# Ten instead of seven pairs of up-projection tiles by seven products of quarters, with the later gated results kept in 32 bits until the down projection

## The chip, the cores and the metric

The kernel runs on one core of one Trainium2 chip. The metric is the device time of one execution in microseconds (us). The kernel before the change took 720.85 us, the median of three runs (719.79 to 722.53).

## The reference, cut to what matters

One decoder layer on `x` of 512 rows and 1024 columns: a token mixer (attention and a state-space scan), a layer norm, and a gated feed-forward part with a second layer norm. The change sits in the feed-forward part, and its scheduling rule reaches the mixer too.

```python
def conv_ffn(h, w_up, conv_w, conv_b, w_down):
    u = causal_dwconv(h @ w_up, conv_w, conv_b)
    g, val = jnp.split(u, 2, axis=-1)
    return (jax.nn.silu(g) * val) @ w_down
...
        h = x * (1.0 + sc2) + sh2
        y = conv_ffn(h, ffn_up_w[i], ffn_conv_w[i], ffn_conv_b[i], ffn_down_w[i])
        x = layer_norm(DEEPNORM_ALPHA * x + (1.0 + g2) * y, ln2_g[i], ln2_b[i])
```

`w_up` is 1024 x 5632: 22 gate tiles and 22 value tiles of 128 columns. `w_down` is 2816 x 1024.

## The kernel before, in words

**Precision.** Every large product is made in three matmuls of a reduced 32-bit type: each operand is split into a high part (`hi`, a copy on ACT) and a low part (`lo`, a subtraction on DVE), and `mm3` multiplies high by high, high by low and low by high. In the trace `wh` and `wl` are the parts of a weight tile, `h2h` and `h2l` those of the normed input, and the two halves of a `mid` tile those of a gated result.

**Up stage.** The 22 pairs (a gate tile `i = 0` and a value tile `i = 1` of one `j`) are made one after the other. A direct pair takes 2 x 8 x 3 = 48 matmuls of 128 x 512 (`up` in the trace). A pair in the list `SEVEN` (before: j = 3, 5, ..., 15) treats weights and input as 2 x 2 quarters and takes seven products of quarters instead of eight: 7 x 4 x 3 = 84 matmuls of 128 x 256 (`sP`, in four PSUM banks). It wants four extra sums of weight quarters (`sw`, DVE), seven splits of weight quarters (`wq`: ACT, then DVE), two copies (`m`, ACT) and seven sums of results (DVE, on `sP` and `u`). The sums of the input (`TS`, name `ts`) are made once and held in four of the six buffers of class "e".

**After a pair.** `up_post` runs a three-tap convolution (one ACT and two DVE instructions per tile), a SiLU on ACT and the product on DVE. In the kernel before it then splits the result at once into a `mid` tile (ACT, then DVE), which the down stage reads.

**Down stage.** `by_tile` makes the output in two passes over the two column halves. Each pass goes through 11 weight items, each of which serves two values of j; an item is 24 matmuls of 128 x 512 for all four row tiles (`dn`). `ln2` adds the residual: `x_back` brings the normed rows back from DRAM into two "e" buffers (`XN`), `row_loads` scales and shifts them on POOL (16 instructions, key `res`), and `ln2` wants them when the first pass ends.

**What sets the order.** The program is written by a greedy planner (`Order`, lines 48 to 300). Work is given as threads; at each step the planner estimates when the next instruction of each thread could start (`start`, `price`) and emits the earliest, with priorities. The result is one fixed order for each engine. Which parts of a tile depend on each other is told by `touch`: for a large SBUF tile by blocks of 128 columns, and before the change for every PSUM tile as one whole (the key set is `{0}`), so that a reader of a part counts as waiting for all that is written to the bank. This is the planner's picture only. The waits in the program are set apart from it, by the framework. Buffers come from classes ("e": 6, "b": 25) and quotas (`R.limit`): `w2` is the number of weight parts of the up stage that may be held, `raw` the number of loaded weight tiles. All loads are issued by SP, in one queue.

Line 300 of the profile is the planner's `emit`, so all instructions share that line and are told apart by the names of their tiles.

Of the kernel before, what the change touches and what calls it, by code (L numbers as in the profile page):

```python
# [9 lines left out]
F32 = mybir.dt.float32  # L10
F32R = mybir.dt.float32r
# [5 lines left out]
P = 128  # L17
SEQ = 512
# [25 lines left out]
class Region:  # L44


    def __init__(self, base=0.0):
        self.base, self.wr, self.rd, self.psum = base, {}, {}, False

    def end(self):  # L50
        return max([self.base] + [v[0] for v in self.wr.values()] + [v[0] for v in self.rd.values()])
# [56 lines left out]
class Order:  # L108
# [37 lines left out]
    def try_alloc(self, a):  # L146
        if a.after:
            if self.due(a) > self.time:
                return None
            a.after = ()  # L150
        pool, slots = self.pools[a.cls]
        group = a.group or a.cls
        if self.used.get(group, 0) >= self.quota.get(group, 1000):
            return None
        free = [s for s in slots if s["free"]]
        if not free:
            return None
        s = min(free, key=lambda q: q["end"])
        t = pool.tile(a.shape, a.dt, name=self.name(a.name), tag=s["tag"], bufs=1)
        s["free"] = False  # L160
        self.used[group] = self.used.get(group, 0) + 1
        self.regs[t.tensor.name] = Region(s["end"])
        self.regs[t.tensor.name].psum = a.cls == "ps"
        self.owner[t.tensor.name] = (s, group)
        return t

# [7 lines left out]
    def touch(self, ap):  # L174
        name = ap.tensor.name
        if name not in self.regs:
            return None
        if name.startswith("dr"):
            return name, [(0, 0)]
        dims = [tuple(d) for d in ap.ap]  # L180
        pitch = max(dims[0][0], 1)
        p0, off = divmod(ap.offset, pitch)
        n = dims[0][1] if dims[0][0] else 1
        if pitch <= self.GRAIN or self.regs[name].psum:
            chunks = {0}
        else:
            starts = [off]
            for st, cnt in dims[1:-1]:
                starts = [s + st * i for s in starts for i in range(cnt if st else 1)]
            st, cnt = dims[-1] if len(dims) > 1 else (0, 1)  # L190
            chunks = {c for s in starts for c in range(s // self.GRAIN, (s + st * (cnt - 1)) // self.GRAIN + 1)}
        keys = [(h, c) for h in range(p0 // 64, (p0 + n - 1) // 64 + 1) for c in chunks]
        return name, keys
# [211 lines left out]
def layer_kernel(  # L405
# [274 lines left out]
            rows_item(w_out, k, n)  # L680
    UP0 = len(items)
    NSPLIT = 4
    SEVEN = [3, 5, 7, 9, 11, 13, 15]
    for j, i in up_tiles:
        cols_item(w_up, i * D_FF + j * P)
    for n in range(2):
# [547 lines left out]
            R.free(XN[t // 2])  # L1234

    def x_back():
        yield Need("tsfree")
        for h in range(2):
            XN[h] = yield buf("e", [P, 2, DM], "XN")
            for i in range(2):  # L1240
                yield S.dma_start(XN[h][:, i], xn_d[2 * h + i])
                R.mark(("back", 2 * h + i))
# [79 lines left out]


    MID, U, E8 = {}, {}, {}
    MTAGS = ["b"] * 12 + ["e"] * 8 + ["b"] * 2

    def conv3(ps, dst, ch, neg):
        f0, f1, f2 = (nfw[:, i, ch - NFF:ch - NFF + 1] if neg else w[:, ch:ch + 1] for i, w in enumerate((fw0, fw1, fw2)))
# [5 lines left out]
    def up_post(j, i, ps, neg=False):  # L1334
        u = yield buf("s", [P, SEQ], "u")
        yield from conv3(ps, u, j + 22 * i, neg)
        if i == 0:
            yield A.activation(u, u, AF.Silu)
            U[j] = u
            R.mark(("u", j))  # L1340
            return
        yield Need(("u", j))
        g = U.pop(j)
        yield V.tensor_mul(g, g, u)
        R.free(u)
        if MTAGS[j] == "b":
            mid = yield buf("b", [P, 2, SEQ], "mid", "mid", F32R)
        else:
            if j % 2 == 0:
                E8[j] = yield buf("e", [P, 2, 2, SEQ], "mid2", dt=F32R)  # L1350
                R.mark(("mid2", j))
            yield Need(("mid2", j - j % 2))
            mid = E8[j - j % 2][:, j % 2]
        yield A.activation(mid[:, 0], g, AF.Copy)
        yield V.tensor_sub(mid[:, 1], g, mid[:, 0].bitcast(F32))
        R.free(g)
        MID[j] = mid
        R.mark(("mid", j))


    RES = {}
# [246 lines left out]
    def seven(j):  # L1608

        h2h, h2l = H2["hl"]  # L1610
        for _ in range(2):
            w_next()
        ps = []
        for i in range(2):
            ps.append((yield bank("gemm", "sP")))

        def b(k0, c):
            return h2h[:, k0:k0 + 4, c], h2l[:, k0:k0 + 4, c]

        def t(m):  # L1620
            return TS[m][:, 0], TS[m][:, 1]

        yield Need("ts")

        for m, p, c, (rh, rl) in ((0, 0, L, b(0, L)), (1, 1, L, t(0)), (2, 0, H, t(1)), (4, 1, H, t(2)),
                                  (5, 2, L, b(4, L)), (6, 3, L, t(3)), (3, 2, H, b(4, H))):
            if p == len(ps):
                ps.append((yield bank("gemm", "sP")))
            yield Need(("ws", j, m))
            w = WS.pop((j, m))  # L1630
            lead[0] += 2 / 7
            for k in range(4):
                yield mm3(ps[p][:, c], w[:, 0, k], w[:, 1, k], rh[:, k], rl[:, k], k == 0, k == 3)
            R.free(w)
            if m == 0:
                R.spawn(seven_out(j, ps), 2)
            R.mark(("sm", j, m))
# [26 lines left out]
    def ffn():  # L1664
        h2h, h2l = H2["hl"]
        pend = []
        for part in range(2):
            c0, c1 = part * 256, part * 256 + 256
            for j, i in up_tiles[:NSPLIT]:
                if part == 0:  # L1670
                    key, n_ = w_next()
                    ps = yield bank("gemm", "up")
                    yield Need(key)
                    w = W.pop(n_)
                    pend.append((ps, w))
                else:
                    ps, w = pend.pop(0)
                for k in range(KC):
                    yield Need(("h2", 2 * part, k // 4), ("h2", 2 * part + 1, k // 4))
                    yield mm3(ps[:, c0:c1], w[0][:, k], w[1][:, k], h2h[:, k, c0:c1], h2l[:, k, c0:c1],  # L1680
                              k == 0, k == KC - 1)
                if part == 1:
                    R.free(*w)
                    R.spawn(up_post(j, i, ps), 2)
        R.free(ROWS.pop("g1p"))
        R.limit(raw=3, w2=10, gemm=8)
        for n, (j, i) in enumerate(up_tiles[NSPLIT:]):
            if j in SEVEN:
                if i == 0:
                    yield from seven(j)  # L1690
                if j == SEVEN[-1] and i == 1:
                    R.free(*TS)
                    R.mark("tsfree")
                    R.limit(w2=7)
                continue
            key, n_ = w_next()
            ps = yield bank("gemm", "up")
            yield Need(key)
            w = W.pop(n_)
            for k in range(KC):  # L1700
                yield mm3(ps, w[0][:, k], w[1][:, k], h2h[:, k], h2l[:, k], k == 0, k == KC - 1)
            R.free(*w)
            R.spawn(up_post(j, i, ps), 2)
        R.free(h2h, h2l)
        RES["rw"] = yield buf("h", [P, 4, DM], "RW")
        RES["w"] = yield buf("h", [P, 4, 2, 512], "wlast", dt=F32R)
        R.mark("fin")
        R.limit(gemm=8, w2=8)
        ps = {}
        cuts = [[(0, 512), (512, DM)]] * 3 + [[(0, 512), (512, 768), (768, DM)]]  # L1710
        for n in range(2):
            for t in range(NT):
                for c in cuts[t][1:] if n else cuts[t][:1]:
                    ps[t, c[0]] = yield bank("gemm", "dn")
                if n == 0:
                    R.spawn(ln2(t, ps, cuts[t]), 0.5 if t == NT - 1 else 1)

            def block(i, tile, w):
                t, (c0, c1) = tile
                s, c = slice(t * P, (t + 1) * P), slice(c0 - n * 512, c1 - n * 512)  # L1720
                for b in range(2):
                    k = 2 * i + b
                    yield Need(("mid", k))
                    yield mm3(ps[t, c0][:, :c1 - c0], MID[k][:, 0, s], MID[k][:, 1, s],
                              w[0][:, b, c], w[1][:, b, c], k == 0, k == NFF - 1)

            tiles = [(t, c) for t in range(NT) for c in (cuts[t][1:] if n else cuts[t][:1])]
            yield from by_tile(tiles, NFF // 2, (1, LATE_DN)[n], block, lambda tile: ("y2", tile[0], tile[1][0]))
# [30 lines left out]
    R.spawn(ada_last(), 8)  # L1759
    R.spawn(quarters(), 1.5)  # L1760
    R.spawn(x_back(), 6)
    R.run()


# [28 lines left out]
```

## Time and profile before

| | us |
|---|---|
| median of three runs (lowest, highest) | 720.85 (719.79, 722.53) |
| profiled execution: device time | 723.08 |
| profiled execution: span | 721.3 |
| busy PE / DVE / ACT / POOL in the span | 703.3 / 584.5 / 342.3 / 58.5 |

The span runs from the first to the last instruction of the profiled execution; 1.78 us of its device time lie around it. Busy times are unions of an engine's instructions. PE matmuls overlap in the records, so a PE that is shown busy may still have small gaps in it. In the chain of waits a row such as `408.36 9.95 PE sP L300 x84` is a stretch of time (start, length, engine, tile name, line, number of instructions).

### The profile page before, as it was taken

The numbers are of one execution on the slowest core, as the hardware profiler recorded it, in microseconds if no ns is written. First come the engines' busy times: TensorE is split into PE (matmuls) and PEld (weight loads), VectorE is DVE, ScalarE is ACT, GpSimd is POOL, SyncE is SP. The second block draws the span as 40 slices with busy tenths as digits, with TensorE's granted clock in tenths as the row PEclk, the third lists the DMA queues.
The fourth block names the chain that finished last, engine by engine and source line by source line (L and its number), as shares of the span: only waits on it lengthen the run. The fifth ranks groups of instructions, "written<-read, shape, count | busy, mean of one in ns | idle before, by whom it ended". The sixth has DMA issues, their size and how long they took to land.

```text
span 721.3 us, 10347 instructions
## 1 busy us (share of the span) xinstructions
PE 703.3 (98%) x3873; PEld 589.1 (82%) x3873; DVE 584.5 (81%) x1072; ACT 342.3 (47%) x605; POOL 58.5 (8%) x71
## 2 busy tenths in 40 slices
PE   8999999999999899999999999999999999999995
PEld 7787887888778787878998888999988888888885
DVE  5879989999898889678899999999985663247646
ACT  2347578655665364323775655556554352211200
POOL 0010012100000000000100000000000019200023
PEclk9999999999999999999999999999999999999998
DMA  8997083063556415654533432444383345322202
GB/s 264 307 286 231 0 264 93 2 175 101 176 162 221 130 30 174 218 190 147 164 100 108 127 98 79 144 149 146 112 268 89 94 153 179 100 88 75 100 30 87
DMA packets 112323, 102.12 MB, mean 142 GB/s; under 512 B 3732, under 2 KB 93200, under 8 KB 112273
## 3 DMA queue, kind: packets, MB, share of 16 engines
q1 hardware_dynamic: 112273, 101.47, 46.0%
q8 instruction: 30, 0.49, 0.3%
q14 instruction: 20, 0.16, 0.1%
HBM read 97.22 MB, written 4.23 MB: 141 GB/s over the span
## 4 chain that ended last, share of the span: by engine, by line
PE 64%; DVE 18%; DMA 6%; SPq 4%; ACT 4%; issue 3%; POOL 0%; DVEq 0%; ACTq 0%
PE up L300 19%; PE dn L300 17%; PE sP L300 9%; PE po L300 7%; PE fm L300 7%; SPq L300 4%; DVE wl L300 3%; DMA ad<-in_ada_w_dram 3%; DVE acc L300 2%; DMA aw<-in_ada_w_dram 2%; DVE Y L300 1%; DVE pr L300 1%; ACT csb L300 1%; DVE u L300 1%; DMA csb<-drcs 1%
## 5 line engine op out<-in xcount | busy, mean ns | idle before, releaser
L300 DVE TENSOR_TENSOR wl<-raw,wh 128x1024 fp32r<-128x1024 f32 x88 | 110.8, 1262 | 51.3 <-ACT wh L300 51.2
L300 ACT ACTIVATE wh<-raw 128x1024 fp32r<-128x1024 f32 x88 | 91.9, 1053 | 83.7 <-PE dn L300 41.0
L300 PE MATMUL dn<-wh,mid 128*128 128x512 f32 (+1 forms) x356 | 102.5, 371 | 0.0
L300 PE MATMUL up<-h2l,wh 128*128 128x512 f32 (+1 forms) x272 | 100.0, 368 | 0.0
L300 PE MATMUL up<-h2h,wh 128*128 128x512 f32 (+1 forms) x272 | 100.0, 368 | 0.0
L300 PE MATMUL up<-h2h,wl 128*128 128x512 f32 (+1 forms) x272 | 100.0, 368 | 0.0
L300 PEld LDWEIGHTS dn<-wh,mid 128*128 128x128 f32 x356 | 64.5, 188 | 12.5
L300 PE MATMUL fm<-hh,wh 128*128 128x512 f32 x176 | 72.5, 412 | 0.0
L300 PE MATMUL fm<-hh,wl 128*128 128x512 f32 x176 | 69.6, 396 | 0.0
L300 PE MATMUL fm<-hl,wh 128*128 128x512 f32 x176 | 69.6, 396 | 0.0
L300 PE MATMUL dn<-wl,mid 128*128 128x512 f32 (+1 forms) x178 | 66.0, 371 | 0.0
L300 PEld LDWEIGHTS up<-h2h,wl 128*128 128x128 f32 x272 | 51.1, 188 | 9.1
L300 PEld LDWEIGHTS up<-h2h,wh 128*128 128x128 f32 x272 | 51.2, 188 | 8.8
L300 PEld LDWEIGHTS up<-h2l,wh 128*128 128x128 f32 x272 | 51.1, 188 | 8.9
L300 DVE SCALAR_TENSOR_TENSOR u<-up,fprm,u 128x511 f32<-128x511 f32 (+1 forms) x60 | 44.6, 746 | 7.6 <-ACT u L300 6.8
L300 DVE SCALAR_TENSOR_TENSOR acc<-ad,csil,acc 128x1024 f32<-128x1024 f32 x28 | 35.8, 1280 | 13.4 <-DMA ad<-in_ada_w_dram 13.2
L300 POOL TENSOR_TENSOR XN<-XN,l 128x512 f32<-128x512 f32 x16 | 25.8, 1630 | 234.7 <-PE up L300 234.1
L300 PE MATMUL sP<-ts,wq 128*128 128x256 f32 x336 | 42.3, 280 | 0.2 <-ACT m L300 0.2
L300 PE MATMUL po<-wh,os 128*128 128x512 f32 x128 | 42.4, 396 | 0.0
L300 PEld LDWEIGHTS sP<-ts,wq 128*128 128x128 f32 x336 | 40.8, 188 | 0.5 <-ACT m L300 0.4
L300 PEld LDWEIGHTS fm<-hh,wl 128*128 128x128 f32 x176 | 33.2, 189 | 7.7
L300 PEld LDWEIGHTS fm<-hh,wh 128*128 128x128 f32 x176 | 33.3, 189 | 7.2 <-issue 0.7
(264 smaller groups left out, 1385.1 us busy)
## 6 DMA issues: line engine op xcount, KB each, us to landing
raw<-in_ffn_up_w_dram SPq DMA_DIRECT2D x44, 512.0 KB
ad<-in_ada_w_dram SPq DMA_DIRECT2D x32, 512.0 KB
raw<-in_mix_in_w_dram SPq DMA_DIRECT2D x26, 512.0 KB
raw<-in_ffn_down_w_dram SPq DMA_DIRECT2D x22, 512.0 KB
aw<-in_ada_w_dram SPq DMA_DIRECT2D x32, 256.0 KB
raw<-in_mix_out_w_dram SPq DMA_DIRECT2D x12, 512.0 KB
csb<-drcs SPq DMA_DIRECT2D x8, 512.0 KB
wr<-in_mix_in_w_dram SPq DMA_DIRECT2D x8, 392.0 KB
```

Source lines behind the costliest of these rows:

```text
L300: getattr(self.hw[op.eng], op.fn)(*op.args, **op.kw)
```

## The change

Three more pairs (j = 17, 19, 21) are made by seven products. The product of gate and value for j = 12 to 21 is written to `KEEP` buffers as one 32-bit piece, and a new thread `keep` splits it into `mid` tiles when the last up matmul has been emitted (`fin`). So the input sums `TS` stay until then, and the rows of the residual come back only as the first two `KEEP` buffers fall free (`kfree`), no longer when `TS` does (`tsfree`). The quota `w2` is 9 throughout the rest of the up stage (before: 10, and 7 after j = 15). In the planner, `touch` takes the whole-bank rule for `sP` tiles alone; other PSUM tiles count by blocks of 128 columns.

```diff
@@ -161,6 +161,7 @@
         self.regs[t.tensor.name].psum = a.cls == "ps"
+        self.regs[t.tensor.name].whole = a.name == "sP"
...
-        if pitch <= self.GRAIN or self.regs[name].psum:
+        if pitch <= self.GRAIN or self.regs[name].whole:
             chunks = {0}
...
-    SEVEN = [3, 5, 7, 9, 11, 13, 15]
+    SEVEN = [3, 5, 7, 9, 11, 13, 15, 17, 19, 21]
...
     def x_back():
-        yield Need("tsfree")
         for h in range(2):
+            yield Need(("kfree", h))
             XN[h] = yield buf("e", [P, 2, DM], "XN")
...
-    MTAGS = ["b"] * 12 + ["e"] * 8 + ["b"] * 2
+    NMID = 12
+    KEEP, KEPT = {}, {}
...
+        if j >= NMID:
+            yield Need(("keep", (j - NMID) // 4))
+            k = KEPT[j] = KEEP[(j - NMID) // 4][:, (j - NMID) % 4]
+            yield V.tensor_mul(k, g, u)
+            R.free(g, u)
+            R.mark(("kept", j))
+            return
         yield V.tensor_mul(g, g, u)
         R.free(u)
...
+    def keep():
+
+        yield Need("tsused")
+        for i in range(2):
+            KEEP[i] = yield buf("e", [P, 4, SEQ], "keep")
+            R.mark(("keep", i))
+        KEEP[2] = yield buf("b", [P, 2, SEQ], "keep", "mid")
+        R.mark(("keep", 2))
+        yield Need("fin")
+        for j in range(NMID, NFF):
+            if j < NMID + 8:
+                if j % 2 == 0:
+                    E8[j] = yield buf("e", [P, 2, 2, SEQ], "mid2", dt=F32R)
+                mid = E8[j - j % 2][:, j % 2]
+            else:
+                mid = yield buf("b", [P, 2, SEQ], "mid", "mid", F32R)
+            yield Need(("kept", j))
+            yield A.activation(mid[:, 0], KEPT[j], AF.Copy)
+            yield V.tensor_sub(mid[:, 1], KEPT[j], mid[:, 0].bitcast(F32))
+            MID[j] = mid
+            R.mark(("mid", j))
+            if j in (NMID + 3, NMID + 7, NFF - 1):
+                R.free(KEEP[(j - NMID) // 4])
+                R.mark(("kfree", (j - NMID) // 4))
...
-        R.limit(raw=3, w2=10, gemm=8)
+        R.limit(raw=3, w2=9, gemm=8)
...
-                if j == SEVEN[-1] and i == 1:
-                    R.free(*TS)
-                    R.mark("tsfree")
-                    R.limit(w2=7)
                 continue
...
-        R.free(h2h, h2l)
+        R.free(h2h, h2l, *TS)
...
+    R.spawn(keep(), 1)
```

Three places show what this does to the order of the instructions. On PE, at the change from pair 16 to pair 17 late in the up stage, the order before has (`up` is the bank of a direct tile, `wh` and `wl` its weight parts):

```order
L300 MATMUL up_5376<-h2h_2780,wh_5262 128x512
L300 MATMUL up_5376<-h2l_2781,wh_5262 128x512
L300 MATMUL up_5376<-h2h_2780,wl_5263 128x512
L300 MATMUL up_5419<-h2h_2780,wh_5303 128x512
L300 MATMUL up_5419<-h2l_2781,wh_5303 128x512
L300 MATMUL up_5419<-h2h_2780,wl_5304 128x512
```

and the changed order has, at the same place (`sP` is a bank of a pair by seven products, `wq` a split quarter of the weights):

```order
L301 MATMUL up_5366<-h2h_2815,wh_5251 128x512
L301 MATMUL up_5366<-h2l_2816,wh_5251 128x512
L301 MATMUL up_5366<-h2h_2815,wl_5256 128x512
L301 MATMUL sP_5415<-h2h_2815,wq_5326 128x256
L301 MATMUL sP_5415<-h2l_2816,wq_5326 128x256
L301 MATMUL sP_5415<-h2h_2815,wq_5326 128x256 x2
L301 MATMUL sP_5415<-h2l_2816,wq_5326 128x256
```

Pair 17 is now 84 matmuls of half the width; pairs 19 and 21 likewise, so direct pairs and pairs by seven alternate to the end of the up stage.

On DVE, around the end of the up stage, the changed order has (`keep` is a 32-bit result, `mid` its low part, `u` a convolution of pair 21, `wl` a part of a down weight):

```order
L301 TENSOR_TENSOR sP_5927<-sP_5927,u_1151_5910 128x256
L301 TENSOR_TENSOR mid_1173_5989<-keep_3846,mid_1173_5989 128x512 x2
L301 SCALAR_TENSOR_TENSOR u_5973<-sP_5946,nfw_92,u_5973 128x511
L301 TENSOR_TENSOR mid_1180_6018<-keep_3846,mid_1180_6018 128x512
L301 SCALAR_TENSOR_TENSOR u_5973<-sP_5946,nfw_92,u_5973 128x510
L301 TENSOR_TENSOR mid_1180_6018<-keep_3846,mid_1180_6018 128x512
L301 SCALAR_TENSOR_TENSOR u_6006<-sP_5927,fprm_90,u_6006 128x511
L301 TENSOR_TENSOR mid_1181_6037<-keep_3847,mid_1181_6037 128x512
L301 SCALAR_TENSOR_TENSOR u_6006<-sP_5927,fprm_90,u_6006 128x510
L301 TENSOR_TENSOR wl_6050<-raw_5920,wh_6049 128x1024
L301 TENSOR_TENSOR mid_1181_6037<-keep_3847,mid_1181_6037 128x512
L301 TENSOR_TENSOR keep_3848<-u_6006,u_5973 128x512
```

Ten splits that stood in the up stage now stand at the start of the down stage; the first `KEEP` buffer is free after the fourth of them, the second after the eighth, which is two rows further on.

On SP the four loads of the residual rows `XN` stood in front of the last seven up weights. They now stand among the down weights: two behind the seventh down weight and the parameter rows, one down weight, the other two, and then the rest of the down weights.

In the mixer the same instructions are emitted in another order from about the first decay sums on. On ACT, before (`pcs` is the bank of those sums, `csT` and `dtot` are read from parts of it, `Y` and `th` belong to the convolution of the scan):

```order
L300 ACTIVATE csT_939<-pcs_929 64x128
L300 ACTIVATE Y_659<-fm_880,prm_76 128x512
L300 ACTIVATE th_948<-Y_659 128x512
L300 ACTIVATE wh_956<-raw_666 128x1024
L300 ACTIVATE dtot_87<-pcs_929 128x64
L300 ACTIVATE dec_88<-dec_88 128x64
```

and changed:

```order
L301 ACTIVATE csT_939<-pcs_929 64x128
L301 ACTIVATE dtot_87<-pcs_929 128x64
L301 ACTIVATE dec_88<-dec_88 128x64
L301 ACTIVATE Y_659<-fm_880,prm_76 128x512
L301 ACTIVATE th_951<-Y_659 128x512
L301 ACTIVATE wh_967<-raw_666 128x1024
```

The readers of a part of a bank move ahead of other work, and from here on the two orders of the mixer differ in many places.

## Rows read from the trace of the kernel before

**Rows 1.** The page: the span, the busy time of each engine, and the shares of the chain of waits by engine and by line.

```profile
span 721.3 us, 10347 instructions
PE 703.3 (98%) x3873; PEld 589.1 (82%) x3873; DVE 584.5 (81%) x1072; ACT 342.3 (47%) x605; POOL 58.5 (8%) x71
...
PE 64%; DVE 18%; DMA 6%; SPq 4%; ACT 4%; issue 3%; POOL 0%; DVEq 0%; ACTq 0%
```

**Rows 2.** The chain of waits in order of time, from the second pair by seven products to the end of the down stage: start us, length us, engine, tile name, line, instructions.

```profile
408.36 9.95 PE sP L300 x84
418.30 11.14 PE up L300 x48
429.45 9.99 PE sP L300 x84
439.44 11.17 PE up L300 x48
450.61 10.12 PE sP L300 x84
460.73 11.20 PE up L300 x48
471.93 9.85 PE sP L300 x84
481.79 11.16 PE up L300 x48
492.95 9.96 PE sP L300 x84
502.90 11.11 PE up L300 x48
...
591.45 122.64 PE dn L300 x594
```

**Rows 3.** Busy time by stretch: start:end, length, then busy us (instructions) of PE, PEld, DVE, ACT and POOL, the granted clock of PE, the DMA share and GB/s. The first five rows are one pair by seven and one direct pair each.

```profile
408.36:429.45 21.09, 21.09 (x134) 18.96 (x134) 20.82 (x35) 11.77 (x19) 0.00 (x0) 1.00 0.45 125
429.45:450.61 21.16, 21.16 (x134) 19.01 (x134) 21.02 (x35) 11.89 (x20) 0.00 (x0) 1.00 0.26 76
450.61:471.93 21.32, 21.32 (x134) 19.02 (x134) 20.92 (x34) 12.07 (x19) 0.00 (x0) 1.00 0.42 124
471.93:492.95 21.02, 21.02 (x135) 18.89 (x134) 20.78 (x34) 11.52 (x19) 0.00 (x0) 1.00 0.40 126
492.95:514.01 21.06, 21.06 (x134) 18.98 (x134) 20.78 (x34) 11.89 (x20) 0.00 (x0) 1.00 0.42 125
```

**Rows 4.** The same view for the mixer (60 to 300 us) and for the first pass of the down stage up to the first read of its result.

```profile
60.00:300.00 240.00, 234.73 (x1345) 188.90 (x1344) 215.85 (x468) 141.59 (x306) 15.78 (x21) 0.99 0.42 130
...
591.45:649.10 57.65, 57.65 (x250) 46.70 (x250) 23.52 (x18) 13.59 (x15) 25.79 (x16) 1.00 0.42 131
```

**Rows 5.** Groups of instructions between 408.36 and 535 us, shapes apart: line, engine, operation, tiles, shapes, count, busy us, mean ns of one, idle us before them and what ended it.

```profile
L300 DVE SCALAR_TENSOR_TENSOR acc<-ad,csil,acc 128x1024 f32<-128x1024 f32 x7 | 9.0, 1279 | 0.0
...
L300 DVE TENSOR_TENSOR mid<-u,mid 128x512 fp32r<-128x512 f32 x12 | 8.2, 684 | 0.1
...
L300 ACT ACTIVATE mid<-u 128x512 fp32r<-128x512 f32 x12 | 7.6, 632 | 9.2 <-DVE u L300 9.1
```

**Rows 6.** DVE in order of time in the first pass of the down stage: start us, length us, engine, line, operation, tiles, shapes, count, and in brackets the idle time before and what ended it.

```profile
603.45 2.35 DVE L300 TENSOR_TENSOR wl<-raw,wh 128x1024 fp32r<-128x1024 f32 x1 [3.88 <-ACT wh L300]
...
620.14 1.23 DVE L300 TENSOR_TENSOR wl<-raw,wh 128x1024 fp32r<-128x1024 f32 x1 [3.40 <-ACT wh L300]
625.72 1.23 DVE L300 TENSOR_TENSOR wl<-raw,wh 128x1024 fp32r<-128x1024 f32 x1 [4.35 <-ACT wh L300]
631.29 1.23 DVE L300 TENSOR_TENSOR wl<-raw,wh 128x1024 fp32r<-128x1024 f32 x1 [4.35 <-ACT wh L300]
...
649.14 0.68 DVE L300 TENSOR_TENSOR y<-dn,RW 128x512 f32<-128x512 f32 x1
```

**Rows 7.** POOL in order of time in the same stretch, columns as in rows 6.

```profile
591.48 26.41 POOL L300 TENSOR_TENSOR XN<-XN,l 128x512 f32<-128x512 f32 x16 [234.09 <-PE up L300]
```

**Rows 8.** A place in order of time where a part of a PSUM bank is read: the decay sums (`pcs`, three products into one bank; `csT` reads the columns of the first). Columns as in rows 6.

```profile
87.81 0.43 PE L300 MATMUL pcs<-tri,da 128*64 128x128 f32 x2
...
88.44 0.39 PE L300 MATMUL pcs<-dd,ones_r 128*128 128x64 f32 x2
88.87 0.27 ACT L300 ACTIVATE csT<-pcs 64x128 f32<-64x128 f32 x1 [3.43 <-PE pcs L300]
```

**Rows 9.** The same view of a state product (`pst`, three products into one bank, two records each; the copy `st` reads the columns of the first).

```profile
120.77 0.94 PE L300 MATMUL pst<-xe,sc 128*128 128x128 f32 x6 [0.37 <-DVE xe L300]
121.74 0.28 ACT L300 ACTIVATE st<-pst 128x128 f32<-128x128 f32 x1 [1.65 <-PE pst L300]
```

**Rows 10.** The same view of the transposes of the normed rows (`pt`, two banks of four transposes; `hk` reads one transpose at a time).

```profile
336.70 1.04 PE L300 MATMUL pt<-ident,XN 128*128 128x128 f32 x8
337.40 1.05 DVE L300 TENSOR_SCALAR hk<-pt,mcol 128x128 f32<-128x128 f32 x3 [1.29 <-PE pt L300]
```

**Rows 11.** The longest single wait of PE in the mixer, in order of time.

```profile
248.48 1.31 PE L300 MATMUL pn<-ones_r,z 128*128 128x1 f32 x8 [1.94 <-DVE mx L300]
```

More of the change, by code (lines that the diff above doesn't have):

```diff
@@ L47, in __init__ @@
     def __init__(self, base=0.0):
-        self.base, self.wr, self.rd, self.psum = base, {}, {}, False
+        self.base, self.wr, self.rd, self.psum, self.whole = base, {}, {}, False, False
     def end(self):
@@ L1343, in up_post @@
         g = U.pop(j)
+        if j >= NMID:
[5 more added lines that the diff above has]
+            return
         yield V.tensor_mul(g, g, u)
         R.free(u)
[L1346 to L1353, printed above, removed]
+        mid = yield buf("b", [P, 2, SEQ], "mid", "mid", F32R)
         yield A.activation(mid[:, 0], g, AF.Copy)
@@ L1358, in up_post @@
         R.mark(("mid", j))
+    def keep():
[12 more added lines that the diff above has]
+            else:
+                mid = yield buf("b", [P, 2, SEQ], "mid", "mid", F32R)
+            yield Need(("kept", j))
[6 more added lines that the diff above has]
+                R.mark(("kfree", (j - NMID) // 4))
     RES = {}
@@ L1623, in seven @@
         yield Need("ts")
+        R.mark("tsused")
         for m, p, c, (rh, rl) in ((0, 0, L, b(0, L)), (1, 1, L, t(0)), (2, 0, H, t(1)), (4, 1, H, t(2)),
```

## The prediction, on record before the changed kernel ran

> **What bounds the kernel now.** I read the page first: PE is busy in 703.3 of 721.3 us, DVE in 584.5, and the chain of waits lies on PE for 64% of the span [rows 1]. These are averages, so the stages come next. In the up stage the chain in order of time is PE alone, stretch after stretch, a direct pair (48 matmuls) behind a pair by seven products (84) [rows 2]. The stretches with one pair of each kind show how near DVE is: 20.82 to 21.02 us of 21.02 to 21.32 [rows 3]. PE sets the time there and DVE would be next, about 0.3 us behind in each stretch. The down stage is PE alone too, 122.64 us [rows 2], with DVE busy in 23.52 and ACT in 13.59 of the 57.65 us of its first pass [rows 4]. The mixer is different: PE shows 234.73 us busy in 240, so it waits visibly for 5.27 us, and DVE is busy in 215.85 [rows 4]. So a change in the up stage is paid in PE time, one in the down stage is hidden as long as it stays short, and a new order in the mixer can go either way.
>
> **The seven products.** The five pairs by seven take 9.95, 9.99, 10.12, 9.85 and 9.96 us, mean 9.974; the five direct pairs between them take 11.14, 11.17, 11.20, 11.16 and 11.11, mean 11.156 [rows 2]. One pair changed is worth 11.156 - 9.974 = 1.182 us of PE, three are worth 3.55 us. That is all on the path, provided that nothing else becomes late.
>
> **DVE and ACT beside them.** A pair by seven needs more from DVE (sums and splits of quarters, sums of results), so the last five pairs, direct until now, come to the load of rows 3: mean 104.32 / 5 = 20.86 of 21.13 us per two pairs, the sum of that column. Two things are taken from it from j = 12 on: two splits of results at 0.684 us each, 1.37 us, and after the last of the seven `acc` steps, each 1.279 us, those too [rows 5]. That leaves at most 20.86 - 1.37 = 19.5 us in 21.13. I take 0 for DVE, with 1.6 us per two pairs as the cover. ACT has 12.07 of 21.32 us at most [rows 3] and loses two splits of 0.632 us [rows 5]; also 0. One `w2` buffer less than before still holds the seven quarters of a pair and both parts of the next direct tile (7 + 2 = 9); in the up stage the order of PE is the same as before up to pair 15 but for one small product. I take 0; were I wrong there, rival 2 is what it would cost.
>
> **The splits moved to the down stage.** Ten splits are 10 x 0.684 = 6.8 us of DVE and 10 x 0.632 = 6.3 us of ACT [rows 5]. They come to a pass in which DVE has 57.65 - 23.52 = 34.1 us free and ACT 44.1 [rows 4]. The first of them is needed by the seventh weight item. Items follow each other every 5.57 us (the low parts at 620.14, 625.72 and 631.29 [rows 6]), so that is 6 x 5.57 = 33 us after the stage begins. Even 24 DVE instructions at 0.7 us, all that stands up to the last split, are 17 us. The low parts of the weights are queued behind some of these; four of them are made before the stage begins, the fifth stands among the splits and is needed after 22 us. Price 0.
>
> **The residual rows, which come back later.** Before, POOL worked on them from 591.48 for 26.41 us, right as the down stage began [rows 7]. Now the first two loads wait for the fourth split, some 4.6 us of DVE work into the stage (four splits at 0.684, two convolution steps and a sum), and the second two for the eighth, some 11 us in. One megabyte at the 131 GB/s which the stretch shows [rows 4] takes 8 us, so an estimate for the start of POOL is 5 + 8 = 13 us into the stage, and for its end 13 + 26.4 = 39.4. The first read of the result stands 649.14 - 591.45 = 57.7 us in [rows 2, 6]. Slack 18 us, price 0. What is queued behind these loads on SP are down weights, the first of them for the eighth item, needed at 39 us; 0 as well. POOL beside DVE makes a low part take 2.35 in place of 1.23 us [rows 6], 1.1 us more in an item of 5.57, also covered.
>
> **The new order of the mixer.** No instruction is added there and none goes; a few copies change between ACT and DVE, with both signs. The planner now believes that a reader of a part of a bank need not wait for the rest. The rows say that it must. `csT` reads what the first product wrote by 87.81 + 0.43 = 88.24, but starts at 88.87, 0.04 after the last product into that bank ends (88.44 + 0.39) [rows 8]. `st` starts at 121.74, 0.03 after the end of all six records [rows 9]. `hk` starts 0.70 us after the first of eight transposes, that is, after the four of its bank [rows 10]. So the planner's picture gets worse at these places by 0.63 us for `csT`, by 121.74 - (120.77 + 0.43) = 0.54 us for each of eight `st`, and by three transposes, 3 x 1.04 / 8 = 0.39 us, for each of eight banks of `hk`: 0.6 + 4.3 + 3.1 = 8.0 us in all. Not one of these is a longer wait by itself: the program waited for the whole bank before too. What it costs is that an early reader stands at the head of ACT's or DVE's queue with other work behind it. Against that stands that a greedy plan gets a new draw, and the old one has waits such as the 1.94 us of `pn` for DVE [rows 11]. The bounds are 8.0 us lost and the 5.27 us that PE visibly waits gained. I take 0, between the two, since the same work is done and nothing in the rows favours either order.
>
> The Trainium skill, page "PSUM — Partial Sum Buffer", section "PSUM bank collisions raise a hardware error", gives the rule "Semaphore-guard PSUM by bank × quadrant (by bank is the simple version), not by address". By that rule the narrower picture is wrong wherever a part is read, and the sum is that of the third rival below. The trace agrees on the wait, by the 0.04 and 0.03 us of rows 8 and 9; it does not show what the order built on it costs.
>
> **The sum.** The profiled execution takes 723.08 us, 721.3 of them span; 723.08 - 3.55 = 719.5. It lies 2.23 us above the median of the runs, 720.85, so I forecast 720.85 - 3.55 = 717.3 us. A measurement of this kernel can tell about 0.5% from no change, 3.6 us, so "faster" ends at 717.25: the forecast lies on that border.
>
> **Rivals.**
>
> 1. *The new order of the mixer is a better draw.* It takes half of the 5.27 us that PE visibly waits there [rows 4], 2.6 us: 717.3 - 2.6 = 714.7. For it: single long waits that can fall away [rows 11]. Against it: DVE is busy in nine tenths of that stage [rows 4], so there is little room to move work into.
>
> 2. *The seven products do not pay late in the up stage.* DVE, or a missing `w2` buffer, becomes the bound, and three pairs cost what direct ones cost: 717.3 + 3.55 = 720.85. For it: DVE is 0.3 us behind PE per two pairs [rows 3]. Against it: the 1.37 us taken from each of those stretches [rows 5], and that PE's stretches show the same length five times [rows 2].
>
> 3. *Early readers block queues in the mixer* (slower). The place is ACT and DVE from 60 to 340 us, the price up to the 8.0 us worked out above: 717.3 + 8.0 = 725.3. At half of it the time is 721.3. It decides, that is, the change turns slower than before, when more than 3.55 of the 8.0 us reach PE. For it: DVE is nearly full, so what it loses PE soon waits for. Against it: most of the readers have work of PE before and after them that is not tied to them.
>
> 4. *The residual rows come too late*, PE's second pass waits for a bank that the residual sum must free. It takes effect once POOL ends more than 18 us later than estimated, and then 1 us for 1 us; with 25 us late, 717.3 + 7 = 724.3. Against it: the slack above.
>
> **How the numbers follow.** Forecast, with the mixer within 2 us of before (715.3 to 719.3): 0.56. Rival 1: 0.18, rival 2: 0.07, rival 3: 0.14, rival 4: 0.05. Faster by over 0.5% are rival 1 and a little over half of the forecast, 0.18 + 0.30 = 0.48. Slower by over 0.5% (724.45 and more) is the upper end of rivals 3 and 4, 0.07. The rest, 0.45, is within 0.5%. The range goes from 714.0, just below rival 1, to 721.4, the half price of rival 3, and leaves out about 0.08 below and 0.1 above.
>
> **What the changed profile would show.** The chain would hold ten stretches of 84 `sP` matmuls of about 10 us up to the start of `dn`, with no `up` stretch of more than 48; from the start of the second `sP` stretch to the first `dn` it would be 183.1 us (591.45 - 408.36 [rows 2]) less 3.55, that is 179.5. DVE would be busy in 19.5 us or less per two pairs at the end of it. `dn` would stay at 122.6 us. POOL would work on `XN` from 10 to 15 us after the first `dn` and end before the first `y`. The start of the first `sP` against before gives the mixer's part alone. The forecast is wrong if that start moves by more than 2 us, if `up` or `sP` stretches lengthen, or if PE waits in the down stage.

## The result, and the profile after

The changed kernel takes 712.88 us (median of four runs, 712.18 to 714.30), the kernel before, on the same chip, 721.69 (719.79 to 723.87). The ratio is 0.988, with a 95% interval of 0.9846 to 0.9913: 8.8 us faster. The forecast was 717.3 and the range began at 714.0, so the prediction was wrong, on the good side. The profiled execution of after took 712.18 us, 710.5 of them span. Its page, the lines that answer to [rows 1]:

```profile
span 710.5 us, 10648 instructions
...
PE 697.4 (98%) x3981; PEld 591.2 (83%) x3981; DVE 603.0 (85%) x1121; ACT 349.4 (49%) x625; POOL 60.0 (8%) x71
...
PE 83%; DVE 12%; issue 2%; ACT 1%; DMA 1%; SPq 0%; DVEq 0%; ACTq 0%
```

PE runs more matmuls and is busy for less time, and the chain lies on PE for 83% in place of 64%. The chain in order of time, answering to [rows 2] (start us, length us, engine, tile, line, instructions):

```profile
421.88 9.83 PE sP L301 x84
431.71 11.15 PE up L301 x48
442.86 9.95 PE sP L301 x84
...
516.57 6.92 PE up L301 x30
523.95 4.18 PE up L301 x18
528.13 10.07 PE sP L301 x84
538.21 11.15 PE up L301 x48
549.36 9.91 PE sP L301 x84
559.26 11.12 PE up L301 x48
570.38 9.92 PE sP L301 x84
580.31 122.92 PE dn L301 x594
```

The last three pairs by seven cost what the first ones did, 9.9 to 10.1 us. From the third pair by seven to the down stage it was 591.45 - 429.45 = 162.00 us before [rows 2]; now it is 580.31 - 421.88 = 158.43, which is 3.57 less. (From the first `sP` on it is 205.37 and 202.13, 3.24 less: the first two pairs took 0.3 us more.) The down stage has not moved (122.92 against 122.64). But the up stage also begins earlier: the first `sP` starts at 378.01 us against 385.92, so 7.9 us were won before it, in the mixer. Busy time there, answering to the first of [rows 4], with the same columns:

```profile
60.00:300.00 240.00, 239.41 (x1379) 194.04 (x1378) 220.57 (x471) 142.28 (x305) 17.53 (x21) 1.00 0.45 142
```

PE's visible idle time is 0.59 us where it was 5.27. That is 4.7 of the 7.9 us. Another part is in the last column but two: the granted clock is 1.00 where it was 0.99. Before, it fell right behind the long wait of [rows 11]. Here are the windows of before around that wait (columns as in [rows 3]):

```profile
246.40:248.40 2.00, 0.14 (x1) 0.00 (x0) 1.96 (x7) 0.00 (x0) 0.00 (x0) 1.00 0.73 243
248.40:250.00 1.60, 1.52 (x9) 1.52 (x10) 1.56 (x7) 0.22 (x1) 0.00 (x0) 0.73 0.00 0
250.00:252.00 2.00, 2.00 (x6) 1.41 (x6) 1.29 (x7) 0.41 (x1) 1.04 (x1) 0.50 0.00 0
252.00:254.00 2.00, 2.00 (x14) 1.82 (x13) 1.90 (x12) 0.87 (x2) 0.00 (x0) 0.86 0.02 4
```

PE shows as busy in nearly all of the last three, but at 0.50 it runs at the lower of its two levels, 1.2 of 2.4 GHz; 0.73 and 0.86 are windows with a part at either level. What is lost is, as an estimate, the length times the part not granted: 1.60 x 0.27 + 2.00 x 0.50 + 2.00 x 0.14 = 1.7 us. So this one wait cost about 3.6 us, not 1.94. Idle time and clock make 6.4 of the 7.9 us. The two orders of PE part at 90 us, and there the profiles are still only 0.16 us apart (90.12 and 89.96), so nearly all of the other 1.5 us lies behind that point, in gaps that the busy share does not show. Not all of the 7.9 us need be the change: one profiled execution stands on each side, and with the very same order of the mixer another one (e2 below) reached the first `sP` 2.1 us later than before did.

The moved work did what was forecast. POOL's row (answering to [rows 7]), and the read of a part of a bank (to the last of [rows 8]):

```profile
593.78 25.93 POOL L301 TENSOR_TENSOR XN<-XN,l 128x512 f32<-128x512 f32 x16 [243.99 <-DVE mid L301]
```

```profile
88.29 0.39 PE L301 MATMUL pcs<-dd,ones_r 128*128 128x64 f32 x2
...
88.72 0.27 ACT L301 ACTIVATE csT<-pcs 64x128 f32<-64x128 f32 x1 [3.42 <-PE pcs L301]
```

POOL begins 13.5 us into the down stage and ends 39.4 us into it. `csT` still starts 0.04 us after the last product into its bank.

### The profile page after: what moved, and what is told of

The parts are those of the page before. It is cut to its first block, busy times and chain, and to the rows that moved or that the text cites. A ratio compares the mean times of both kernels' runs of the same rounds, so it can differ in the third digit from the quotient of the medians.

```text
span 710.5 us, 10648 instructions
## 1 busy us (share of the span) xinstructions
PE 697.4 (98%) x3981; PEld 591.2 (83%) x3981; DVE 603.0 (85%) x1121; ACT 349.4 (49%) x625; POOL 60.0 (8%) x71
## 4 chain that ended last, share of the span: by engine, by line
PE 83%; DVE 12%; issue 2%; ACT 1%; DMA 1%; SPq 0%; DVEq 0%; ACTq 0%
PE dn L301 17%; PE fm L301 14%; PE up L301 13%; PE sP L301 11%; PE po L301 9%; PE first L301 5%; PE tm L301 3%; DVE u L301 2%; DVE wl L301 2%; DVE acc L301 1%; PE py L301 1%; PE pov L301 1%; PE psS L301 1%; DVE wq L301 1%; PE pT L301 1%
## 5 line engine op out<-in xcount | busy, mean ns | idle before, releaser
L301 PE MATMUL up<-h2h,wh 128*128 128x512 f32 (+1 forms) x224 | 81.2, 363 | 0.0
L301 PE MATMUL up<-h2h,wl 128*128 128x512 f32 (+1 forms) x224 | 81.1, 362 | 0.0
L301 PE MATMUL up<-h2l,wh 128*128 128x512 f32 (+1 forms) x224 | 81.1, 362 | 0.0
L301 PE MATMUL sP<-ts,wq 128*128 128x256 f32 x480 | 60.0, 281 | 0.2 <-ACT m L301 0.2
L301 PEld LDWEIGHTS sP<-ts,wq 128*128 128x128 f32 x480 | 58.0, 189 | 0.4 <-ACT m L301 0.4
L301 PE MATMUL sP<-h2h,wq 128*128 128x256 f32 x240 | 47.9, 282 | 0.6 <-DVE sP L301 0.6
L301 PEld LDWEIGHTS up<-h2h,wl 128*128 128x128 f32 x224 | 42.2, 188 | 7.2
L301 PEld LDWEIGHTS up<-h2l,wh 128*128 128x128 f32 x224 | 42.1, 188 | 6.8
L301 PEld LDWEIGHTS up<-h2h,wh 128*128 128x128 f32 x224 | 42.1, 188 | 6.6
L301 PEld LDWEIGHTS sP<-h2h,wq 128*128 128x128 f32 x240 | 39.0, 188 | 1.8 <-DVE sP L301 1.0
```

The costliest lines, as they stand in the source:

```text
L301: getattr(self.hw[op.eng], op.fn)(*op.args, **op.kw)
```

## The experiments

The theory after this result: the up stage gained by the products, and the mixer gained because another rule on banks gives the greedy planner another draw, in which fewer long waits of PE fall. Rivals: the narrow picture itself helps, reader by reader; or the moved splits made the up stage faster. All twelve runs and both kernels stand in one table, from one profiled execution each for the starts and the medians of the timed runs for the time. "First sP to dn" is the time from the first `sP` matmul to the first `dn` matmul. Ratios are to before on the same chip. "Mixer" names the order of PE up to the first `sP`; runs with one name there have the same. One name does not mean one start: A's first `sP` came at 384.83 to 387.99 us, C's at 377.60 to 380.03. And a profiled execution need not be a middling one: that of e1 took 718.72 us, 1.6 below its median, those of e2 (724.82) and e10 (713.88) 3.8 and 2.3 above theirs.

| run | mixer | first sP | first sP to dn | median us | ratio to before, 95% |
|---|---|---|---|---|---|
| before | A | 385.92 | 205.37 | 721.69 | |
| after | B | 378.01 | 202.13 | 712.88 | 0.9846 to 0.9913 |
| e1_rule | B | 378.85 | 207.67 | 720.33 | 0.9944 to 0.9991 |
| e2_pairs | A | 387.99 | 205.10 | 721.06 | 0.9974 to 1.0014 |
| e3_pcs | C | 377.82 | 205.73 | 715.76 | 0.9893 to 0.9938 |
| e4_pst | D | 386.33 | 205.62 | 722.74 | 0.9999 to 1.0032 |
| e5_seven | B | 378.92 | 205.82 | 716.29 | 0.9872 to 0.9940 |
| e6_both | C | 377.60 | 207.98 | 716.06 | 0.9871 to 0.9936 |
| e7_wait | B | 386.45 | 202.09 | 719.65 | 0.9938 to 0.9979 |
| e8_drawb | E | 383.13 | 205.75 | 719.59 | 0.9938 to 0.9976 |
| e9_drawa | F | 386.02 | 203.40 | 722.36 | 0.9986 to 1.0026 |
| e10_late | C | 380.03 | 202.02 | 711.59 | 0.9839 to 0.9886 |
| e11_early | B | 378.00 | 205.76 | 715.82 | 0.9893 to 0.9930 |
| e12_pairs_late | A | 384.83 | 201.96 | 718.04 | 0.9919 to 0.9963 |

**The two halves, each alone.** e1_rule is before with only the new rule on banks; e2_pairs is after with the old rule.

```diff
+        self.regs[t.tensor.name].whole = a.name == "sP"
-        if pitch <= self.GRAIN or self.regs[name].psum:
+        if pitch <= self.GRAIN or self.regs[name].whole:
```

> The kernel before with the narrow rule alone: seven pairs by seven products, splits at once, and the mixer's order of the changed kernel. Theory: the two parts of the change are separate, and the mixer's order is worth what the start of the first sP matmul shows, 385.7 - 377.8 = 7.9 us; with 720.85 to 721.7 for before that is 713 to 714 us, and the first sP near 378. Rival (the pairs pay more than their 3.55 us, and the mixer's start moved only because the profiled execution of before was a long one): 717 us or more.

```diff
-        self.regs[t.tensor.name].whole = a.name == "sP"
+        self.regs[t.tensor.name].whole = a.cls == "ps"
```

> The changed kernel with the whole-bank rule for every PSUM tile: ten pairs, late splits, and the mixer's order of the kernel before. Theory: only the three pairs' 3.3 to 3.55 us are left, 717.3 to 718.3 us, with the first sP near 385.7 and the long waits of PE at 184, 207 and 246 us back. Rival (pairs pay more): 714 us or less.

e1's first `sP` came at 378.85, so the rule alone carries the mixer's order, as after has it. Yet the whole was only 720.33, and e2 721.06, both outside what the theory expected (713 to 714 and 717.3 to 718.3): -1.9 and -1.1 us, each against before on its own chip, where both together make -8.8. A part was lost again between the first `sP` and `dn`, which was 2.3 us longer in e1 than in before and 3 us longer in e2 than in after. For e2 that is about all; e1's profile still has 7.1 - 2.3 = 4.8 us on before's, of which its median shows 1.9. Something in the up stage was not part of either theory; the last three runs below are about it.

**One reader at a time.** Before, with the narrow rule for `pcs` alone (e3), then for `pst` alone (e4).

```diff
+        self.regs[t.tensor.name].whole = a.cls == "ps" and a.name != "pcs"
```

> The kernel before with the narrow rule for the bank of the decay sums (pcs) alone. If the narrow picture helps reader by reader, this has a part of the 7.9 us, and with the next run the two parts sum to about 7.9: 714 to 721 us. If it is only another draw of a greedy plan, it lands anywhere, 713 to 725 us, and the two do not sum.

```diff
+        self.regs[t.tensor.name].whole = a.cls == "ps" and a.name != "pst"
```

> The kernel before with the narrow rule for the banks of the state products (pst) alone. Reader by reader: the rest of the 7.9 us, 714 to 721 us. Another draw: anywhere from 713 to 725 us, the two gains not adding up to that of the narrow rule for all.

A single bank, read twice, brings the first `sP` as early as the whole rule (377.82; 715.76 us, which fits both expectations; PE busy in 238.18 of 240 us of the mixer). Eight banks of `pst` bring nothing: 722.74, outside the 714 to 721 of the sum over readers. In e4 one wait took the place of several. PE's row in order of time, then the windows behind it:

```profile
271.81 0.80 PE L301 MATMUL psS<-qk 128*128 128x512 f32 x1 [5.50 <-DVE mx L301]
```

```profile
272.00:274.00 2.00, 2.00 (x5) 1.63 (x6) 1.96 (x6) 0.58 (x3) 0.00 (x0) 0.50 0.69 231
274.00:276.00 2.00, 2.00 (x6) 1.54 (x6) 1.95 (x7) 0.99 (x2) 0.00 (x0) 0.50 0.44 143
276.00:278.00 2.00, 2.00 (x8) 1.59 (x7) 1.29 (x4) 1.35 (x5) 0.00 (x0) 0.67 0.31 119
```

A wait of 5.50 us, and another 4.00 x 0.50 + 2.00 x 0.33 = 2.7 us at half clock behind it. That speaks for a draw and against a sum over readers.

**A draw without any rule.** The planner's assumed delay behind a TensorE write is put from 0.19 to 0.20 us, in before (e8) and in after (e9). Nothing else is touched.

```diff
-    LAT = dict(PE=0.19, V=0.18, A=0.2, G=0.16, S=1.0)
+    LAT = dict(PE=0.20, V=0.18, A=0.2, G=0.16, S=1.0)
```

> The kernel before, with the planner's delay behind a TensorE write put at 0.20 us in place of 0.19: no rule on banks is touched, no instruction is added or left out. Theory (new draw): the mixer's order differs and the first sP moves by 2 to 8 us either way, most likely earlier since before's mixer holds four waits of over 0.7 us; time 714 to 724. Rival (the rule on banks itself made the mixer of after shorter): nothing of it here, the first sP within 1.5 us of 385.9 and the time within 1.5 us of 721.7.

> The kernel after, with the planner's delay behind a TensorE write put at 0.20 us in place of 0.19: a new draw of the mixer under after's rules; the two neighbouring loads of ad stand where after has them. Theory (a draw counts by its waits, and after's mixer, with 0.59 us of visible PE idle from 60 to 300, has next to none left to lose): the first sP comes at 377 to 384, not earlier than 377; first sP to dn 202.1; time 712 to 719. Rival (the narrow rule for sP makes the mixer short by itself): the first sP within 1 us of 378.0, the time within 1 us of 712.9.

e8 moves the first `sP` by 2.8 us, as the draw has it and beyond the rival's 1.5. (A's own three executions spread over 3.2 us, but the timed runs agree: 719.59 against 722.76 for before on the same chip.) e9 is the strongest single run: after's rule on banks, all of after's instructions, one planner constant moved by 0.01 us, and the mixer's gain is gone (first `sP` 386.02, time 722.36, both above the ranges expected). Its page of waits and its window say where:

```profile
PE pT L301 <- DVE z L301: 4.0, 1, 4.0
```

```profile
240.00:300.00 60.00, 55.70 (x307) 44.56 (x306) 49.48 (x116) 30.26 (x60) 2.37 (x2) 0.97 0.39 122
```

One wait of 4.0 us, and the clock at 0.97 over the 60 us around it. The rival, that the narrow rule makes a short mixer by itself, falls. Two orders under each rule (B and F, A and E) do not say which rule is better on the average. In six orders of the mixer the first `sP` came between 377.6 and 388.0.

**What a long wait costs.** After, with six copies of `z` onto itself ahead of `pn`; the orders of PE, DVE and SP stay.

```diff
         pn = yield bank("mix", "pn", [sq])
+        if g == 0:
+            for _ in range(6):
+                nc.scalar.activation(sq, sq, AF.Copy)
```

> The kernel after, with six copies of z onto itself on ACT (0.5 us each, the values stay) ahead of the first pn, where the order of PE, DVE and SP stays as it is: PE has to wait some 2 to 3 us at pn near 247 us, as before did there for 1.94 us. Theory (a wait of this size is paid twice, once by itself and once by the half clock behind it): the granted clock falls to 0.50 for 2 to 5 us behind the wait, and the time grows by the wait and another 1.4 to 2.5 us, in all 3.5 to 5.5: 716.4 to 718.4. Rival (only the wait counts): 2 to 3 us, 714.9 to 715.9. Rival (the plan has slack that takes it up later): under 1 us.

The wait came at the other `pn`, at 275 us, and was 3.37 us. PE's row, and the windows from the wait on:

```profile
278.83 1.44 PE L301 MATMUL pn<-ones_r,z 128*128 128x1 f32 x6 [3.37 <-ACT z L1183]
```

```profile
278.90:280.00 1.10, 1.10 (x6) 1.10 (x6) 0.00 (x0) 1.10 (x4) 0.00 (x0) 0.50 0.00 0
280.00:282.00 2.00, 2.00 (x8) 1.71 (x8) 1.27 (x2) 0.80 (x1) 1.03 (x1) 0.50 0.00 0
282.00:284.00 2.00, 2.00 (x6) 1.61 (x5) 1.13 (x6) 1.43 (x3) 0.96 (x1) 0.50 0.41 78
284.00:286.00 2.00, 2.00 (x8) 1.53 (x8) 0.80 (x2) 0.00 (x0) 0.00 (x0) 0.72 0.98 377
```

Half clock for 5.1 us and 0.72 for 2 more is 2.55 + 0.56 = 3.1 us on top of 3.37, 6.5 in all. The medians differ by 719.65 - 712.88 = 6.8 us; set against before on its own chip each, by 8.8 - 3.1 = 5.7. In the profiles the first `sP` is 8.4 us later, with another wait, of 1.0 us, at 207 us. The wait is paid twice, as the theory had it, though 719.65 lies above the 716.4 to 718.4 that it gave for a wait of 2 to 3 us. The rivals "only the wait" (3.4) and "taken up later" fall.

**The products apart from the moved splits.** After with seven pairs by seven.

```diff
-    SEVEN = [3, 5, 7, 9, 11, 13, 15, 17, 19, 21]
+    SEVEN = [3, 5, 7, 9, 11, 13, 15]
```

> The kernel after, with seven pairs by seven products in place of ten; the later up results still stay in one piece. Theory (the up stage gains by the products alone): three direct pairs of 11.15 us in place of three of 9.95, so 3.5 us more than after, about 716.4; first sP to dn 205.6. Rival (what the up stage gained is DVE's lighter queue, since the splits have left it): first sP to dn stays near 202 and the time near 713. In both the mixer is that of after, with the first sP within 1 us of 378.

716.29 and 205.82, against 716.4 and 205.6 expected: the three pairs are worth 3.4 us in the time, 3.7 in the stage. The moved splits, which leave DVE less to do there, alone give the up stage nothing.

**The up stage's own lottery.** e6_both is after with the rule of e3.

```diff
-        self.regs[t.tensor.name].whole = a.name == "sP"
+        self.regs[t.tensor.name].whole = a.cls == "ps" and a.name != "pcs"
```

> The kernel after, with the narrow rule taken from sP alone and given to pcs alone: every other PSUM tile is priced by the whole bank. A third order of the mixer under the same up stage and down stage. Theory (each change of a rule is a new draw of the plan, and what counts is how many waits of over 1 us the draw holds): the mixer may end anywhere between 377 (no such wait) and 388 (before's); with e3's mixer at 378 the time is 712 to 713. Rival (the parts add, reader by reader): pcs alone was worth 6.4 us and the ten pairs 3.4, so 711.5 to 712.5 and the first sP at 378.

The first `sP` is as good as after's, but the way to `dn` takes 207.98 us, and neither theory had that. Three rows of e6 in order of time, of ACT, DVE and PE, and then SP's queue ahead of them:

```profile
471.34 1.06 ACT L301 ACTIVATE wh<-raw 128x1024 fp32r<-128x1024 f32 x1 [4.40 <-DMA raw<-in_ffn_up_w_dram]
```

```profile
472.44 1.23 DVE L301 TENSOR_TENSOR wl<-raw,wh 128x1024 fp32r<-128x1024 f32 x1 [1.74 <-ACT wh L301]
```

```profile
474.66 0.58 PE L301 MATMUL sP<-h2h,wq 128*128 128x256 f32 x1 [2.50 <-DVE sP L301]
```

```profile
458.13 5.91 SPq L301 DMA_DIRECT2D ad<-in_ada_w_dram  x2
464.99 6.13 SPq L301 DMA_DIRECT2D raw<-in_ffn_up_w_dram  x4
```

Read from the last fence back to the first: two loads of `ad` (for the last row of the ada product) stand next to each other ahead of four raw up weights. The weights land later, `wh` waits 4.40 us on ACT, `wl` stands idle at the head of DVE's queue for 1.74 us, and behind `wl` stands the sum into `sP` that frees the bank PE wants. In e1, e2 and e6 the two neighbouring `ad` loads stand at this place; in before and after, and in the other runs up to e9, four raw loads later. e9 shows that their place is not all: with the loads four raw loads later it has 203.40 us, 1.3 more than after, and PE waits there for DVE at `sP` 1.8 us in all. e10 moves the loads back in e6, e12 does the same in e2, and e11 moves them forward in after. The edit moves the whole last ada row, its sums on DVE (`acc`) with its loads. That the loads count and not the sums is read from the rows above, where DVE stands idle ahead of `wl`; no run parts the two.

```diff
-        yield from ada_row(5, "g2r", RES, UP0 + 8)
+        yield from ada_row(5, "g2r", RES, UP0 + 11)
```

> e6_both with the loads of the last ada row started three weight items later (UP0 + 11 for UP0 + 8): the two ad loads that stand side by side on SP move behind the next four raw loads, as after has them. The mixer is that of e6. Theory (two ad loads side by side ahead of a raw hold up wh on ACT, wl and with it the adds into sP on DVE, and PE stands at sP): the waits of sP for DVE go from 3.3 to under 1 us, first sP to dn from 207.98 to 202 to 203, time 716.1 - 5.5 = 710.5, at most 712. Rival (the up stage answers to how the mixer ended, not to the ad loads): first sP to dn stays at 207 to 208, time 715.5 to 716.5.

> e2_pairs (the ten pairs and the kept results under before's rule on banks) with the loads of the last ada row started three weight items later, so that the two neighbouring ad loads stand as in after. Mixer as before. Theory (the ten pairs are worth 3.5 us, and e2 lost them again to the ad loads): first sP to dn 202 to 203, time 721.7 - 3.4 = 718.3 (717.3 to 719.5). Rival (the pairs give their gain only with after's mixer): 205 and more, 720.5 to 721.5.

```diff
-        yield from ada_row(5, "g2r", RES, UP0 + 8)
+        yield from ada_row(5, "g2r", RES, UP0 + 10)
```

> The kernel after with the loads of the last ada row started two weight items later (UP0 + 10 for UP0 + 8), by which the two ad loads that stand side by side come four raw loads earlier, as in e1, e2 and e6. Theory (as for e10, the other way): sP waits for DVE by 2 to 3.5 us more near 470 to 485, first sP to dn from 202.1 to 205 to 208, time 715.5 to 718.5. Rival (the place of these loads does nothing): 202.1 and 712 to 713.5.

All three came out as the theory said. SP's queue in e10, and what PE waits for in e11 (total us, times, longest):

```profile
460.37 0.34 SPq L301 DMA_DIRECT2D ad<-in_ada_w_dram  x1
466.84 5.37 SPq L301 DMA_DIRECT2D raw<-in_ffn_up_w_dram  x4
473.08 14.31 SPq L301 DMA_DIRECT2D ad<-in_ada_w_dram  x2
```

```profile
PE sP L301 <- DVE sP L301: 3.8, 3, 2.3
```

In e10 the stretch goes from 207.98 to 202.02 us and the time from 716.06 to 711.59; in e12 from 205.10 to 201.96 and from 721.06 to 718.04; in e11 the other way, from 202.13 to 205.76 and from 712.88 to 715.82. e10 has the best median of all, but its interval and after's overlap. In the same way a part of e1 can be read (after's mixer, the `ad` loads at the bad place: 720.33 where e5 has 716.29, and 207.67 us in the stretch where e5 has 205.82). That is 1.9 of 4.0 us; e1 was not run with the loads moved, and the rest is open.

The parts add once the `ad` loads stand well: e5 (the mixer's order, without the three pairs) has a ratio of 0.9906, e12 (the pairs without the mixer's order) 0.9941; the product is 0.9848, just inside the interval of after, which begins at 0.9846.

## Why the prediction was wrong

- *Seven products*, -3.55: right. 3.57 us in the chain, 3.4 between e5 and after, 3.8 between e12 and its before. They cost 9.9 to 10.1 us each late in the up stage too. The stretch that the prediction named, from the second `sP` to `dn`, took 580.31 - 399.90 = 180.4 us, not 179.5: PE waits 0.5 us for DVE in it, which before it did ahead of that stretch. Rival 2 did not happen in after; e1, e2, e6 and e11 show that DVE can become late there, in e2, e6 and e11 through SP's queue, of which the prediction saw only the order at the down weights.
- *DVE and ACT beside them*, 0: right. The last two stretches of a pair by seven and a direct one (from 528.13 and 549.36) have 19.89 and 19.21 us of DVE in 21.23 and 21.02, 19.55 in the mean; 19.5 or less was forecast. (The lowest DVE row in [rows 3] is 20.78, not the 20.82 of the prediction's first paragraph; its sum has it right.)
- *Moved splits* and *residual rows*, 0: right. POOL started 13.5 us and ended 39.4 us into the stage, where 13 and 39.4 were estimated, and `dn` took 122.92. That the end agrees to the decimal is luck: POOL began 0.5 us later and took 0.5 us less (25.93 for 26.41). Rival 4 did not happen.
- *The mixer's new order*, taken as 0: this step failed. Rival 1 named what happened, a better draw, but at 2.6 us; it was 7.9 us in the profiles and about 5.4 to 6.5 in the medians (e5: 716.29 against 721.69, or against the 722.76 of its own chip run). Two things were wrong. The bound on a gain, 5.27 us of visible idle time, was too small: it left out the half clock behind a long wait, 1.7 us, which stood in the row of the mixer as 0.99 and was read as nothing. And 0 as the middle value had no support in rows: the outcome depends on whether a wait of 2 to 5 us falls in the draw. Before's order already held one, so there was more to win than to lose: the orders tried reach the first `sP` from 8.3 us earlier to 0.4 us later than before's profile, and up to 2.1 us later where before's own order was run again (e2). The draw that after got, one of the two earliest of six, was luck, as e9 shows.
- *Rival 3*, early readers block queues, 8.0 us: not seen. A planner that believes that a part of a bank can be read early loses nothing by it that these runs could tell from its luck: with that picture for `pcs` the mixer ends at 377.8, with it for `pst` at 386.3. The rule of the Trainium skill, page "PSUM — Partial Sum Buffer", section "PSUM bank collisions raise a hardware error", is to guard PSUM by bank and not by address. The trace agrees in that the waits still go by bank: `csT` starts 0.04 us after the last product.
- *What would show it*: the test named was the start of the first `sP`, wrong if it moved by more than 2 us. It moved by 7.9.

## What to carry to other kernels

Where a greedy planner writes the order, every edit that it can see is a new draw of stages that the edit does not touch: price that draw by the spread of a few neutral variants (a constant moved by 0.01), not by 0, and try some of them before a rule is credited with a gain. A long wait of PE is to be read together with the granted clock in the windows behind it. When two halves of a change do not add, look at the queue that both share, here SP's, before the engines.

## What the runs showed that was not expected

The clock behind a wait fell to half in before (wait 1.94 us), e4 (5.50), e7 (3.37), e9 (4.0) and, in the up stage, e6 (2.50), where it stayed at 0.50 from 474.66 to 478 us; it did not fall in e11 (2.28 us at 474.62, all windows behind it at 1.00). After's own profile has it too, where both orders are still the same: a wait of 1.90 us ends at 9.00 us, and from 11.6 to 15.0 us the clock is 0.50. So the length of the wait alone does not decide whether it falls, and what does was not tried.

Nor does the order decide how long it lasts. Before, e2 and e12 have the same order of the mixer, and in all three PE waits at the same `pn` (1.94, 2.31 and 2.34 us). By the same estimate the clock behind it cost 1.7 us in before and in e12, but 3.4 in e2:

```profile
248.60:250.00 1.40, 0.94 (x5) 0.94 (x5) 1.36 (x5) 0.00 (x0) 0.00 (x0) 0.63 0.00 0
250.00:252.00 2.00, 2.00 (x8) 1.81 (x8) 1.11 (x7) 0.63 (x1) 0.73 (x1) 0.50 0.00 0
252.00:254.00 2.00, 2.00 (x8) 1.60 (x8) 1.61 (x5) 0.05 (x1) 0.32 (x1) 0.50 0.00 0
254.00:256.00 2.00, 2.00 (x9) 1.60 (x8) 1.50 (x12) 0.93 (x2) 0.00 (x0) 0.55 0.01 4
```

That is most of the 2.1 us by which e2's first `sP` comes later than before's. It may be why one program varies more when it holds such waits, which was not followed from run to run: e2 took 718.89 to 724.82 us in ten runs, after 712.18 to 714.30 in four. In e7 a wait of 1.0 us appears at 207 us. The same order has one like it there in e1 and e5 (1.1 and 1.0) and none above 0.4 us in after and e11. Why it comes and goes stays open.
